# A hybrid decoder trunk: five value projections of the first layer moved behind the block inverse, the inverse traced in five parts

## The chip, the cores and the metric

The kernel runs on one core of a Trainium2 chip. The metric is the device time of one execution in microseconds. The engines are named as the profile names them: PE (TensorE; PEld is its weight load), DVE (VectorE), ACT (ScalarE), POOL (GpSimd) and SP (SyncE, whose queue issues the weight loads).

## What is computed

Two decoder layers over 512 positions of width 1024, each with a feed-forward block. The first layer's mixer is a gated DeltaNet with 8 heads, and the change lies in it:

```python
p = h @ w_in                                  # q, k, v, gate, and two rates per head
qkv = silu(causal_dwconv(qkv, conv_w))        # 4 taps
q, k = l2norm(q) * DK ** -0.5, l2norm(k)
Lmat = where(strict, einsum(kb, k) * decay, 0)            # kb = k * beta, per chunk
sol = triangular_solve(eye + Lmat, [v * beta, kb * exp(gc)])   # unit lower triangular
...                                           # state recurrence over the chunks
o = rmsnorm(o, onorm_g) * silu(gate)
return o @ w_out
```

The second layer is a sliding-window attention with sinks, and the work ends with an RMS norm. All of it is float32.

## The kernel before

Activations lie transposed, 128 channels on the partitions and 512 positions along the free axis. A weight matrix is cut into pieces of 128 output channels by 1024 inputs. For each piece, `weights` loads 512 KB into one of three `raw` buffers, ACT casts it to a rounded high part `whi`, and DVE subtracts to get the low part `wlo` (two buffers each). A projection of one piece is 24 products on PE: eight k-tiles of high weights with high and low activations, then eight of low weights with high activations. They accumulate in one of two PSUM tiles named `mm`; six more tiles, `sm`, serve all small products. `next_weights` keeps one further piece loaded and cast.

A piece's sums are evicted by `convolved`: DVE multiplies by R (`u`), ACT scales by the last tap, DVE adds three taps (line 234), ACT applies SiLU (line 634). A gate's piece needs only the eviction (line 650) and a SiLU. A key head (`k_head`) then has its own transposes and products, its decay and a copy of its diagonal blocks to `dg`. A value head (`v_head`) has four transposes on PE, with the value as their operand, and four scaled copies back on ACT, with the coefficients `c1`. The last key head calls `coefficients`, which makes `c1`, `c2n` and their kin on DVE.

`inverse` inverts all 32 by 32 diagonal blocks at once. DVE transposes `dg` into `lan`, POOL multiplies `lan` by the coefficients (line 605), and 31 rounds of one multiplication (line 613) and one addition (line 614) on DVE follow, each needing the one before. Then DVE transposes the result into `Tc` and `Uc` (lines 618 and 619). `place` copies `Uc` into the four diagonal strips of `U`, two on DVE and two on ACT (line 626). `level(h)` is a generator that builds the inverse of a 128 by 128 block of head h out of these, in five steps of small products; its first step copies a piece of `Tc` into `tm` on ACT (line 752), its second has the first matmuls (`tm` with `NT`), its third also needs `U`. Up to three heads are in flight.

The pieces are numbered in the text as `order` runs, from 0. Before, that is eight keys, then values 16, 17, gate 24, values 18, 19, gate 25, values 20, 21, gate 26, value 22, gate 27, value 23, gate 28: 21 pieces, so that piece 11 is value 18. In the middle of each piece from the seventh on, `follow(2)` runs up to two waiting heads, always leaving one. `inverse()` is traced whole after piece 13. Behind the pieces come `place()`, 12 products of the first query, 8 more, and the last value head. `queries` is a generator that yields after each product; it stops at a head's end until `level` has raised `solved` above that head. In the level loop `fill(early, 6)` draws six products after each step of a level.

What sets the order: a planner in the tile framework orders each engine's instructions by the priority of their tracing and by when it expects their inputs, and allocates buffers. `pin` keeps matmuls and transposes of this layer in the order in which they are traced. DVE, ACT and POOL are ordered by the planner. Engines wait for one another by semaphores. The level loop, which the diff does not print in full, is

```python
        while active or h < AH:
            if h < AH and len(active) < 3:
                active.append(level(h))
                h += 1
            for x in list(active):
                if next(x, 0) == 0:
                    active.remove(x)
                fill(early, 6)
```

Of the kernel before, what the change touches and what calls it, by code (L numbers as in the profile page):

```python
# [18 lines left out]
KT = D // P  # L19
NC = S // P  # L20
AH = 8
# [26 lines left out]
def tile_trunk(  # L48
# [48 lines left out]
    def mm(*args, **kw):  # L97
        pin(T.matmul(*args, **kw))  # L98
# [10 lines left out]
    def sm_tile():  # L109
        return psum[1].tile([P, S], F32, tag="sm", name="sm")  # L110
# [223 lines left out]
    with ExitStack() as phase:  # L334
# [3 lines left out]
        def row(tag, name):  # L338
            return dp.tile([P, S], F32, tag=tag, name=name, bufs=8)
# [24 lines left out]
        w_rates = w_rates[:, 0:KT * 48].rearrange("p (k n) -> p k n", n=48)  # L364
        nc.sync.dma_start(raw_ba[:, 0:P], w_ba)

        first_pieces = iter(range(8, 24)), iter(range(24, 29))
        order = [next(first_pieces[kind]) for kind in (0,) * 8 + (0, 0, 1, 0, 0, 1, 0, 0, 1, 0, 1, 0, 1)]
        sources = [w_in[n] for n in order + list(range(8)) + list(range(29, 32))] + [w_out[n] for n in range(KT)]
        ahead = []  # L370

        def next_weights():
# [147 lines left out]
        def squares(dst, h, src):  # L520
            junk = temp("junk")
            for c in range(NC):
                cs = slice(c * P, (c + 1) * P)
                A.activation(junk[:, cs], src[:, cs], AF.Square, accum_out=dst[:, h * NC + c:h * NC + c + 1])
# [11 lines left out]
        kT, kd, NT, vb, qT = [], [], [], [], []  # L536

        def transposed(x):
            pst = sm_tile()
            for c in range(NC):  # L540
                turn(pst[:, c * P:(c + 1) * P], x[:, c * P:(c + 1) * P], ident)
            return pst
# [27 lines left out]
        def q_head(h, q):  # L570

            squares(qss, h, transposed(q))
            pq = sm_tile()
            for c in range(NC):
                mm(pq[:, c * P:(c + 1) * P], kT[h][:, c * P:(c + 1) * P], q[:, c * P:(c + 1) * P], start=True, stop=True)
            V.tensor_tensor(DT[h], pq, DT[h], ALU.mult)
# [23 lines left out]
        def inverse():  # L600

            lan = big("lan", [P, 32, 32])
            V.transpose(lan, dg.rearrange("p hc i -> p i hc"))
            V.transpose(c2t, c2n)
            G.tensor_tensor(lan, lan, c2t.unsqueeze(2).to_broadcast([P, 32, 32]), ALU.mult)
            tmp = big("tmp", [P, 1024])
            tl = big("tl", [P, 32, 32])
            G.memset(tl, 0.0)
            V.memset(tl.rearrange("p a b -> p (a b)")[:, 0:1024:33], 1.0)
            for j in range(31):  # L610
                n = 31 - j
                tv = tmp[:, 0:n * (j + 1)].rearrange("p (i c) -> p i c", c=j + 1)
                V.tensor_tensor(tv, lan[:, j + 1:, j:j + 1].to_broadcast([P, n, j + 1]), tl[:, j:j + 1, 0:j + 1].to_broadcast([P, n, j + 1]), ALU.mult)  # L613
                V.tensor_tensor(tl[:, j + 1:, 0:j + 1], tl[:, j + 1:, 0:j + 1], tv, ALU.add)  # L614

            Tc = big("Tc", [P, HC, 32])
            Uc = big("Uc", [P, HC, 32])
            V.transpose(Tc, tl.rearrange("p i c -> p c i"))
            V.transpose(Uc.rearrange("p a b -> p (a b)"), tl.rearrange("p a b -> p (a b)"))
            G.memset(U, 0.0)  # L620
            Tinv.extend((Tc.rearrange("p c hc -> p hc c"), Uc.rearrange("p i hc -> p hc i")))

        def place():
            for q in range(4):
                qs = slice(32 * q, 32 * q + 32)
                (V.tensor_copy if q < 2 else A.copy)(U[qs, :, qs], Tinv[1][qs])

        unread, after, SG = [], [], []

        def convolved(ps, n, x):  # L630
            u = temp("u")
            V.tensor_tensor(u, ps, R, ALU.mult)
            conv(x, u, col("conv", 4 * n, 4), 4)
            A.activation(x, x, AF.Silu)
# [19 lines left out]
        def follow(n):  # L654
            for _ in range(min(n, len(after) - 1)):
                f, h, x = after.pop(0)
                f(h, x)
# [4 lines left out]
        solved = [0]  # L662

        def queries():
            waits = None
            for h in range(AH):
                w = next_weights()
                ps = mm_tile()
                for i in range(3 * KT):
                    if i == 18 and waits:  # L670
                        q_head(*waits)
                    products(ps, w, i, i + 1)
                    yield
                while solved[0] <= h:
                    yield
                qT.append(row("NT", "q"))
                convolved(ps, h, qT[-1])
                waits = (h, qT[-1])
            for _ in range(24):
                next(late, None)  # L680
                yield
            q_head(*waits)

        def gates():
            while len(SG) < AH:
# [8 lines left out]
        def fill(steps, n):  # L694
            for _ in range(n):
                next(steps, None)

        for i, n in enumerate(order):
            w = next_weights()
            if i == 0:  # L700
                products(ps_first, w, 2 * KT)
                unread.append((ps_first, n))
                continue
            ps = sm_tile() if i == 2 else mm_tile()
            products(ps, w, 0, 12)
            if i == 1:
                y = rms_mean(*parts)
            elif i == 2:
                rates()
            elif i == 6:  # L710
                gc_rows = sums()
            elif i > 6:
                if i == 6 + 1:
                    decays(range(4), gc_rows)
                follow(2)
            products(ps, w, 12)
            unread.append((ps, n))
            if i == 1:
                R = tpool.tile([P, S], F32, tag="R", name="R", bufs=1)
                A.copy(R, rms_bc(y))  # L720
                A.copy(ba, ps_ba[32:48, :])
                V.tensor_tensor(ba, ps_ba[:16, :], ba, ALU.add)
                V.tensor_tensor(ba, ba, R[:16, :], ALU.mult)
            elif i == 6 + 1:
                decays(range(4, 8), gc_rows)
            read()
            if i == 13:
                inverse()
        late = gates()
        early = queries()  # L730
        place()
        fill(early, 12)
        follow(1)
        fill(early, 8)
        after.append(None)
        follow(1)


        def pairs(x):
# [48 lines left out]
        active, h = [], 0  # L788
        while active or h < AH:
# [3 lines left out]
            for x in list(active):  # L793
                if next(x, 0) == 0:
                    active.remove(x)
                fill(early, 6)
        fill(early, 2 * AH * 3 * KT)


        St = None  # L800
# [116 lines left out]
        for m in range(KT):  # L917
            if m < 2:
                ps = two[m][0]
            else:  # L920
                w = next_weights()
                ps = mm_tile()
                for k in range(KT):
                    out_products(ps, w, k)
            h = hpool.tile([P, S], F32, tag="h", name="h")
# [13 lines left out]
    with ExitStack() as phase:  # L939
# [137 lines left out]
        ps, steps = q_steps(0)  # L1077
# [11 lines left out]
        for n in range(32 + 6):  # L1089
            if n < 32:  # L1090
                t, part = n // 4, n % 4
                if part == 0 and t < 7:
                    ps, steps = q_steps(t + 1)
# [11 lines left out]
        for m in range(KT):  # L1105
            hi, lo = weights(w_o[m], KT)
            ps = mm_tile()
# [76 lines left out]
```

## Time and profile before

| | us |
|---|---|
| three runs, median | 1239.77 |
| three runs, lowest and highest | 1237.69 and 1240.0 |
| the profiled execution | 1236.28 |
| its span, first to last instruction | 1234.6 |
| PE busy, of the span | 1215.3 |
| DVE busy, of the span | 822.3 |

All times in the rows are counted from the start of the span. A row of a timeline has the start, the duration, the engine, the line, the operation, what it writes and reads with the shape, and a count where equal instructions follow each other; what stands in square brackets is the engine's idle time before it and who ended it. Matmuls are pipelined: a row's duration is longer than the distance to the next matmul. The granted clock is a share of 2.4 GHz.

### The profile page before, as it was taken

To read this page: it belongs to the slowest core of one execution; us is meant where nothing else is said; L and a number is where in the kernel's file an instruction comes from. 1 tells how busy PE (TensorE), PEld (TensorE's weight loads), DVE (VectorE), ACT (ScalarE), POOL (GpSimd) and SP (SyncE) were. 2 spreads that over 40 slices of the span, in tenths; PEclk is the share of its full clock that TensorE was granted. 3 is DMA by queue.
4 is the path that set the end of the run, shared out by engine and by line. 5 is a ranking of instruction groups with operands and counts; after the bars stand their busy time and mean duration, and the time that the engine had idled before them with its cause. 6 is when DMAs were issued, how large, how long until landed. Compare 5 with 4: busy or idle time off the path is not lost.

```text
span 1234.6 us, 15981 instructions
## 1 busy us (share of the span) xinstructions
PE 1215.3 (98%) x6072; PEld 1008.5 (82%) x6072; DVE 822.3 (67%) x1430; ACT 585.6 (47%) x1146; POOL 50.5 (4%) x97
## 2 busy tenths in 40 slices
PE   9999989999999999999999999999999999999997
PEld 7887777897888888888888878888888888888887
DVE  6899955568586677675333689865876776762243
ACT  6664576465444444443222478754444444432231
POOL 1010000000000000000000003220000000000000
PEclk9999999999999999999999999999999999999999
DMA  5212211222333322332333321112333333333331
GB/s 204 86 51 81 90 52 52 69 70 69 103 92 96 102 90 99 103 96 83 97 99 102 104 74 42 45 49 89 99 89 102 103 87 102 102 89 100 94 94 69
DMA packets 33341, 108.69 MB, mean 88 GB/s; under 512 B 3824, under 2 KB 5360, under 8 KB 33264
## 3 DMA queue, kind: packets, MB, share of 16 engines
q1 hardware_dynamic: 32112, 106.66, 28.0%
q8 instruction: 48, 0.79, 0.3%
q10 hardware_dynamic: 1152, 1.01, 0.2%
q14 instruction: 29, 0.24, 0.1%
HBM read 105.56 MB, written 2.10 MB: 87 GB/s over the span
## 4 chain that ended last, share of the span: by engine, by line
PE 85%; DVE 10%; ACT 3%; issue 1%; DMA 0%; SPq 0%; DVEq 0%; ACTq 0%
PE mm L98 75%; PE sm L98 8%; DVE wlo L120 1%; PE sm L101 1%; DVE v L234 1%; DVE s L1032 1%; DVE tl L614 1%; DVE tmp L613 1%; ACT s L1040 1%; DVE q L1006 1%; DVE s L1043 1%; DVE s L1027 1%; DVE dg L561 0%; ACT whi L119 0%; DMA xk<-in_xT 0%
## 5 line engine op out<-in xcount | busy, mean ns | idle before, releaser
L98 PE MATMUL mm<-xh,whi 128*128 128x512 f32 x968 | 381.2, 394 | 0.0
L98 PE MATMUL mm<-xl,whi 128*128 128x512 f32 x968 | 377.8, 390 | 0.0
L119 ACT CAST whi<-raw 128x1024 fp32r<-128x1024 f32 (+1 forms) x192 | 198.4, 1034 | 357.8 <-PE mm L98 289.0
L120 DVE TENSOR_TENSOR wlo<-raw,whi 128x1024 fp32r<-128x1024 f32 (+1 forms) x192 | 230.0, 1198 | 107.7 <-PE mm L98 59.4
L98 PE MATMUL mm<-xh,wlo 128*128 128x512 f32 x968 | 242.0, 391 | 0.0
L98 PEld LDWEIGHTS mm<-xh,whi 128*128 128x128 f32 x968 | 182.0, 188 | 38.7 <-issue 0.6
L98 PEld LDWEIGHTS mm<-xl,whi 128*128 128x128 f32 x968 | 182.0, 188 | 36.7
L98 PEld LDWEIGHTS mm<-xh,wlo 128*128 128x128 f32 x968 | 181.2, 188 | 37.7
L234 DVE SCALAR_TENSOR_TENSOR y<-u,small,y 128x511 f32<-128x511 f32 (+1 forms) x176 | 131.3, 748 | 3.7 <-ACT y L231 0.7
L98 PE MATMUL mm<-gh,whi 128*128 128x512 f32 x330 | 129.3, 392 | 0.0
L98 PE MATMUL mm<-gl,whi 128*128 128x512 f32 x330 | 129.3, 392 | 0.0
L231 ACT ACTIVATE y<-u,small 128x512 f32<-128x512 f32 x88 | 71.7, 816 | 100.2 <-DVE u L269 100.2
L269 DVE TENSOR_TENSOR u<-mm,R 128x512 f32<-128x512 f32 x88 | 60.3, 687 | 71.1 <-PE mm L98 71.0
L98 PE MATMUL mm<-gh,wlo 128*128 128x512 f32 x330 | 82.8, 391 | 0.0
L98 PEld LDWEIGHTS mm<-gh,wlo 128*128 128x128 f32 x330 | 62.0, 188 | 13.6
L98 PEld LDWEIGHTS mm<-gl,whi 128*128 128x128 f32 x330 | 62.1, 188 | 13.4
L98 PEld LDWEIGHTS mm<-gh,whi 128*128 128x128 f32 x330 | 62.0, 188 | 13.5
L154 DVE TENSOR_TENSOR gl<-y,gh 128x512 fp32r<-128x512 f32 x44 | 30.5, 693 | 50.6 <-ACT gh L153 50.6
L285 DVE TENSOR_TENSOR h<-mm,h 128x512 f32<-128x512 f32 x15 | 10.4, 692 | 45.3 <-PE mm L98 45.3
L1056 POOL TENSOR_SCALAR_AFFINE_SELECT pT<-pT 128x256 f32<-128x256 f32 x64 | 29.8, 467 | 93.1 <-ACT pT L1054 90.8
L274 DVE TENSOR_TENSOR y<-y 128x512 f32<-128x512 f32 x44 | 30.5, 692 | 1.4
L273 ACT ACTIVATE y<-y 128x512 f32<-128x512 f32 x44 | 27.5, 625 | 2.1 <-DVE y L234 2.1
(298 smaller groups left out, 1519.1 us busy)
## 6 DMA issues: line engine op xcount, KB each, us to landing
raw<-in_w_up SPq DMA_DIRECT2D x88, 512.0 KB, 3.5
raw<-in_w_dn SPq DMA_DIRECT2D x32, 512.0 KB, 3.5
raw<-in_w_in SPq DMA_DIRECT2D x31, 512.0 KB, 3.5
raw<-in_w_dn SPq DMA_DIRECT2D x16, 384.0 KB, 3.1
raw<-in_w_out SPq DMA_DIRECT2D x8, 512.0 KB, 3.5
raw<-in_w_q SPq DMA_DIRECT2D x8, 512.0 KB, 3.5
raw<-in_w_o SPq DMA_DIRECT2D x8, 512.0 KB, 3.5
xk<-in_xT SPq DMA_DIRECT2D x8, 256.0 KB, 4.6
```

The costliest lines, as they stand in the source:

```text
L98: pin(T.matmul(*args, **kw))
L101: pin(T.transpose(out, x, eye))
L119: A.copy(hi[:, :w], raw[:, :w])
L120: V.tensor_tensor(lo[:, :w], raw[:, :w], hi[:, :w].bitcast(F32), ALU.subtract)
L154: V.tensor_tensor(lo, src, hi.bitcast(F32), ALU.subtract)
L231: A.activation(dst, u, AF.Identity, scale=last, bias=bias)
L234: V.scalar_tensor_tensor(dst[:, d:], u[:, :S - d], w[:, j:j + 1], dst[:, d:], ALU.mult, ALU.add)
L269: V.tensor_tensor(u, ps, R, ALU.mult)
L273: A.activation(cv[0], cv[0], AF.Silu)
L274: V.tensor_tensor(cv[0], cv[0], cv[1], ALU.mult)
L613: V.tensor_tensor(tv, lan[:, j + 1:, j:j + 1].to_broadcast([P, n, j + 1]), tl[:, j:j + 1, 0:j + 1].to_broadcast([P, n, j + 1]), ALU.mult)
L1056: G.affine_select(out=pT[:, x], in_=pT[:, 0], compare_op=ALU.is_ge, fill=0.0, base=x - 1, pattern=[[0, 2], [-sign, P]], channel_multiplier ...
```

## The change

The first layer's list of pieces ends after value 18 and five gates: keys 8 to 15, values 16 to 18, gates 24 to 28, 16 pieces. Values 19 to 23 become the first five pieces of the `queries` generator, with their heads (`v_head`) traced after the 18th product of the next piece, as the queries' own heads are. `inverse` becomes a generator with four stops, and its five parts are traced after the pieces 11 to 15, the five gates. The 12 and 8 products of the first query that stood between `place()` and the level loop are gone, and the one value head left is traced there. The number of products, and what each computes, stays the same.

```diff
-        first_pieces = iter(range(8, 24)), iter(range(24, 29))
-        order = [next(first_pieces[kind]) for kind in (0,) * 8 + (0, 0, 1, 0, 0, 1, 0, 0, 1, 0, 1, 0, 1)]
-        sources = [w_in[n] for n in order + list(range(8)) + list(range(29, 32))] + [w_out[n] for n in range(KT)]
+        order = list(range(8, 16)) + list(range(16, 19)) + list(range(24, 29))
+        sources = [w_in[n] for n in order + list(range(19, 24)) + list(range(8)) + list(range(29, 32))] + [w_out[n] for n in range(KT)]
...
                 V.tensor_tensor(tl[:, j + 1:, 0:j + 1], tl[:, j + 1:, 0:j + 1], tv, ALU.add)
+                if j % 7 == 6:
+                    yield
...
         def queries():
+
             waits = None
-            for h in range(AH):
+            for n in [*range(19, 24), *range(AH)]:
                 w = next_weights()
                 ps = mm_tile()
                 for i in range(3 * KT):
                     if i == 18 and waits:
-                        q_head(*waits)
+                        waits[0](*waits[1:])
                     products(ps, w, i, i + 1)
                     yield
-                while solved[0] <= h:
+                if n >= 16:
+                    v = row("vb", "v")
+                    convolved(ps, n, v)
+                    waits = (v_head, n - 16, v)
+                    continue
+                while solved[0] <= n:
                     yield
                 qT.append(row("NT", "q"))
-                convolved(ps, h, qT[-1])
-                waits = (h, qT[-1])
+                convolved(ps, n, qT[-1])
+                waits = (q_head, n, qT[-1])
             for _ in range(24):
                 next(late, None)
                 yield
-            q_head(*waits)
+            waits[0](*waits[1:])
...
-            if i == 13:
-                inverse()
+            if i >= 11:
+                if i == 11:
+                    inverting = inverse()
+                next(inverting, None)
         late = gates()
         early = queries()
+        for _ in inverting:
+            pass
         place()
-        fill(early, 12)
-        follow(1)
-        fill(early, 8)
         after.append(None)
-        follow(1)
+        follow(len(after))
...
-        fill(early, 2 * AH * 3 * KT)
+        fill(early, 3 * AH * 3 * KT)
```

## Rows read from the trace of the kernel before

**Rows 1.** The page: busy time of each engine, share, instructions.

```profile
PE 1215.3 (98%) x6072; PEld 1008.5 (82%) x6072; DVE 822.3 (67%) x1430; ACT 585.6 (47%) x1146; POOL 50.5 (4%) x97
```

**Rows 2.** Waits of PE, whole span: total us, times, longest.

```profile
PE sm L101 <- ACT v L634: 5.5, 3, 2.8
...
PE sm L98 <- DVE tm L761: 0.4, 1, 0.4
```

**Rows 3.** Windows: length, busy us and count by engine, granted clock, DMA.

```profile
core 0: us, PE busy (x) PEld busy (x) DVE busy (x) ACT busy (x) POOL busy (x), PEclk, DMA share, GB/s
...
110.00:145.00 35.00, 33.83 (x155) 27.73 (x154) 34.00 (x75) 15.89 (x29) 0.00 (x0) 1.00 0.30 90
...
160.00:242.00 82.00, 81.55 (x602) 65.18 (x601) 45.55 (x72) 46.33 (x139) 3.38 (x10) 1.00 0.18 58
```

**Rows 4.** Timeline of PE: starts of pieces, last value's transposes, first level.

```profile
89.75 0.39 PE L98 MATMUL mm<-xh,whi 128*128 128x512 f32 x1
...
109.28 0.39 PE L98 MATMUL mm<-xh,whi 128*128 128x512 f32 x1
...
114.72 0.39 PE L98 MATMUL mm<-xh,whi 128*128 128x512 f32 x1
...
120.66 0.39 PE L98 MATMUL mm<-xh,whi 128*128 128x512 f32 x1
...
158.22 0.66 PE L101 MATMUL sm<-const,v 128*128 128x128 f32 x4 [2.80 <-ACT v L634]
158.64 1.18 PE L98 MATMUL mm<-xh,wlo 128*128 128x512 f32 x4
159.65 0.81 PE L98 MATMUL sm<-tm,NT 128*96 128x64 f32 x8
```

**Rows 5.** DVE by line, 91.3 to 145.13: busy us, mean ns, idle before.

```profile
L234 DVE SCALAR_TENSOR_TENSOR v<-u,small,v 128x509 f32<-128x509 f32 (+2 forms) x15 | 11.2, 744 | 0.0
L120 DVE TENSOR_TENSOR wlo<-raw,whi 128x1024 fp32r<-128x1024 f32 x9 | 10.9, 1216 | 0.0
L614 DVE TENSOR_TENSOR tl<-tl,tmp 128x31 f32<-128x31 f32 (+15 forms) x31 | 10.6, 341 | 0.7
L613 DVE TENSOR_TENSOR tmp<-lan,tl 128x31 f32<-128x31 f32 (+15 forms) x31 | 10.5, 339 | 0.6
L632 DVE TENSOR_TENSOR u<-mm,R 128x512 f32<-128x512 f32 x5 | 3.4, 683 | 0.0
L650 DVE TENSOR_TENSOR u<-mm,R 128x512 f32<-128x512 f32 x4 | 2.7, 683 | 0.0
```

**Rows 6.** Timelines of POOL, DVE and ACT around the inverse.

```profile
99.71 1.92 POOL L605 TENSOR_TENSOR lan<-lan,c2t 128x1024 f32<-128x1024 f32 x1 [29.71 <-DVE t L164]
...
130.47 0.68 DVE L650 TENSOR_TENSOR u<-mm,R 128x512 f32<-128x512 f32 x1
131.07 0.40 DVE L613 TENSOR_TENSOR tmp<-lan,tl 128x240 f32<-128x240 f32 x1
...
145.13 2.09 DVE L618 STREAM_TRANSPOSE Tc<-tl 128x1024 f32<-128x1024 f32 x1
...
147.26 1.75 ACT L752 COPY tm<-Tc 32x128 f32<-32x128 f32 x4 [2.97 <-DVE Tc L618]
148.92 4.25 ACT L626 COPY U<-Uc 32x1024 f32<-32x1024 f32 x2
```

**Rows 7.** Windows at the end of the span, columns as in rows 3.

```profile
1227.00:1228.00 1.00, 0.84 (x8) 0.60 (x6) 0.80 (x5) 0.00 (x0) 0.00 (x0) 1.00 0.00 0
...
1233.00:1234.00 1.00, 0.00 (x0) 0.00 (x0) 0.00 (x0) 0.00 (x0) 0.00 (x0) 0.50 0.19 68
```

**Rows 8.** Timeline of PE, two of the kernel's first 512-column matmuls.

```profile
5.86 0.63 PE L98 MATMUL sm<-xh,w_rates 128*48 128x512 f32 x1 [0.59 <-DVE w_rates L386]
...
6.99 0.39 PE L98 MATMUL mm<-xl,whi 128*128 128x512 f32 x1
```

**Rows 9.** Timeline of PE in the level loop: a group of six products.

```profile
163.31 0.50 PE L98 MATMUL mm<-xh,whi 128*128 128x512 f32 x1
...
164.89 0.43 PE L98 MATMUL sm<-tm,U 32*32 32x32 f32 x8
```

## The prediction

> **What bounds the kernel now.** I read the page's engine shares first, then TensorE's own waits, then the stretch from 60 to 242 us by windows, and there the timelines of TensorE and VectorE. The shares say that TensorE (PE) is busy 98% of a span of 1234.6 us [rows 1], and the diff removes or adds no matmul. So time can only come from places where PE waits, or go to new ones. PE's list of waits names what this layer can give back: three waits of together 5.5 us on transposes of a value head, each time for the SiLU that ends that value's convolution, and one of 0.4 us in the first block of the inverse's levels [rows 2]. The longest, 2.80 us, is the last value's, at 158.22 [rows 4]. That is 5.9 us in all, and no more can be won here.
>
> The windows say what is behind those waits. From 110 to 145 us VectorE (DVE) is busy 34.0 of 35 us, PE 33.8; from 160 to 242 us DVE is busy only 45.6 of 82, ACT 46.3, and PE practically always [rows 3]. So DVE is the late engine until the inverse is done, and PE afterwards. DVE's work between 91.3 and 145.13 us, grouped by line, is 15 convolution steps, 9 subtractions for weight pieces, 62 steps of the inverse and 9 evictions [rows 5]. The inverse's steps stand there between the others, and none of those groups had more than 0.7 us of idle time ahead of it: DVE is a full queue, and the end of the inverse is the sum of what lies in front of it.
>
> **The change, part by part.** Pieces are numbered as `order` runs, from 0; pieces 0 to 9 and their companions do not change.
>
> *What PE does before the first level.* Before, PE starts piece 11 at 89.75 and the first matmul of a level (tm with NT) at 159.65: 69.90 us, of which 5.50 is waiting, so 64.4 us of work [rows 2, 4]. After, what stands in program order between the same two points is five gates, the transposes of three values and six products. One undisturbed piece of 24 products takes 114.72 - 109.28 = 5.44 us, a product 0.227; a piece with one value's transposes takes 120.66 - 114.72 = 5.94, so those cost 0.50, or about 0.35 where they follow other small matmuls [rows 4]. The sum is 5 x 5.44 + 0.50 + 0.35 + 0.40 + 6 x 0.227 + 0.1 for the switch = 29.9 us. PE stands in front of the first level at 89.75 + 29.9 = 119.7. The other 34.5 us of its work come behind.
>
> *When the first level can start.* It needs Tc, the transposed inverse, and four copies of it on ACT. Before, Tc starts at 145.13 (2.09 us) and the four copies at 147.26 take 1.75, so the operands are there at 149.0, 3.9 us after Tc's start [rows 6]. After, DVE has less in front of Tc. Four values (19 to 22) leave this stretch: 12 of the 15 convolution steps. Durations overlap by 0.08 us: the eviction at 130.47 lasts 0.68, and the next instruction starts after 0.60 [rows 6]. A convolution step of 0.744 us in the mean [rows 5] so counts 0.66, in all 7.9 us. Evictions go from 9 to 6 (one value, five gates): 3 x 0.60 = 1.8 us. Weight subtractions go from 9 to 6, since PE calls pieces 18 to 20 later: 3 x (1.216 - 0.08) = 3.4 us. That is 13.1 us, and Tc starts at 132.0; the first level at 135.9.
>
> *The new wait.* 135.9 - 119.7 = 16.2 us. Before, five value pieces more stood in this stretch, and 18 products more, those of the first query that the two removed `fill` lines put there. Since DVE is full, later or earlier evictions and casts shift nothing else in this sum. Its ends: if the planner runs the inverse ahead of everything that is not needed, it starts where POOL has finished lan, 99.71 + 1.92 = 101.6 [rows 6], takes 62 steps of 0.34 us and the gaps of 1.3 us, 22.4 us [rows 5], and must still let two subtractions and four evictions pass (4.7 us): Tc at 128.7, first level at 132.6, wait 12.9. If one more subtraction and two more evictions go first on DVE (2.3 us), it is 138.2 and 18.5.
>
> *Behind the wait.* Queued behind the blocked matmul on PE are the other levels and all products of the values and queries; nothing else on the chip can feed PE, so every microsecond goes into the total. POOL's clearing of the tm tiles waits for the inverse as before. SP's weight loads run three tiles ahead and then stand still until PE resumes. ACT copies two strips of U in 4.25 us [rows 6] directly behind the first level's operands; the third step of the level needs U, and PE reaches it after 0.6 + 2 x 1.5 us, so 0.6 us of waiting is in it.
>
> *The clock.* After PE's last matmul, at 1227 to 1228 us, the granted clock reads 1.00 (2.4 GHz), and by 1233 it reads 0.50 (1.2 GHz), with no matmul since 1227.8 [rows 7]. In the stretch with PE's longest waits, 2.8 us and less, it reads 1.00 throughout [rows 3]; a wait of 16 us is longer than PE's idleness before that low reading. Back at work the first 512-column matmuls would run at half speed: among the kernel's first matmuls one took 0.63 us at 5.86, and the same shape 0.39 at 6.99 [rows 8]. I estimate from these two rows up to 6 us at half speed, of which half is lost. With the 0.6 us for U, which a slow PE would not notice, I take 2.6 us; ends 0.6 and 2.9. The Trainium skill says the same in "TensorE: Matmul & The Clock Gate", Part 1: the clock starts low, sustained activity releases it, and an idle stretch puts it back; its section on oscillation warns of kernels that pay this at each gap. By that rule the 2.6 us are due; without it the sum would be 2.0 less. The end of this trace agrees with the fall.
>
> *Interleaving.* Six products between two small steps of a level take 164.89 - 163.31 = 1.58 us instead of 1.36 [rows 9]: 0.2 us for the switch. The level loop calls 40 groups of six. Before, 12 of them found the query generator waiting for `solved`, since 168 of the 240 calls became products; after, the values fill all 40. That is 12 x 0.2 = 2.4 us, less about 1.0 for value transposes that no longer split a piece: 1.4, ends 0 and 2.6.
>
> *What I cost at nothing.* The moved DVE and ACT work of five values (3 convolution steps, an eviction, a weight subtraction: about 4 us on DVE; scaling, SiLU, four scaled copies, a cast: 3.5 on ACT) goes to a stretch where both were busy a little over half [rows 3], and which grows by the same 34 us of PE work; at 20 us more each they stay below 66 of some 115. If that cover failed, a late SiLU would cost PE 1 to 3 us, as now [rows 2]. Tracing the inverse in five parts changes what a priority says, but its steps are interleaved already and DVE is full; it moves the time only inside the bounds above.
>
> **The sum.** -5.9 (old waits) + 16.2 (new wait) + 2.6 (clock, U) + 1.4 (switches) = +14.3 us. The profiled execution took 1236.28 us, 1.7 around its span; the three runs have a median of 1239.77, 0.28% more. By the profiled one the result is 1250.6, by the median 1254.1. I forecast 1254.
>
> **Rivals.**
> (a) The inverse runs ahead, or the clock stays up. With the early end of 12.9 us for the wait and the low ends of the clock, -5.9 + 12.9 + 0.6 + 1.4 gives +9.0, so 1249; with the profiled base and no switches, 1244. For it: the first parts of the inverse are traced earlier than any later gate. Against it: evictions and casts of the gates are traced earlier still. Chance 0.18.
> (b) More stands ahead of Tc, or value heads wait in the level loop as they do now: 18.5 instead of 16.2 and up to 2 us of SiLU waits: +18, 1258. Chance 0.10.
> (c) Not slower: products of the values overtake the blocked level on PE. Place: PE's queue behind the last gate. The two accumulators and two ready weight pieces would let 48 products go, and more as DVE evicts. It takes 16.2 + 1.4 - 5.9 = 11.7 us of cover, 52 products beyond the six, to reach the old time; if the whole 16.2 were covered, the result would be -4.5, 1235. Against it: `pin` keeps program order, and in the trace PE sat 2.80 us in front of the last transposes with four products of the same query ready right behind them [rows 4]. The Trainium skill, "TensorE: Matmul & The Clock Gate", Part 2, agrees: only weight loads are pulled ahead, matmuls stay in order. Chance 0.06.
> My own case has 0.66.
>
> **Range and chances.** Own case and (b) reach from 1249 to 1259, and (a) down to 1244; so 1244 to 1259. A measurement of this kernel can tell about 0.2% (2.5 us) from no change. Faster by more than that is two thirds of (c): 0.04; within it 0.02; slower 0.94.
>
> **What the new profile would show.** Right: one wait of PE of 13 to 18 us in front of the first tm matmul with NT, ended by ACT's copies of Tc, which end near 136; the three waits on value transposes gone; granted clock below 1.00 in the microseconds after it; the last 96 products in one run after the levels. Tc's start tells the DVE sum: 132 by mine, 129 if the inverse ran ahead. Wrong: if PE executes products between the last gate and the first level in numbers (case c), or if the stretch from the last gate to the levels is short because Tc starts before 120, which would mean that DVE's queue in front of the inverse was not what I counted.

## The result and the profile after

| | before | after |
|---|---|---|
| four runs of each, median, us | 1239.88 | 1256.91 |
| lowest and highest, us | 1237.69 to 1240.72 | 1256.59 to 1257.46 |
| the profiled execution, us | 1236.28 | 1257.46 |
| its span, us | 1234.6 | 1255.7 |

The changed kernel takes 1.0146 times as long, with a 95% interval of 1.0131 to 1.0161: 17.0 us more by the medians, 21.2 by the two profiled executions. The forecast was 1254, in a range of 1244 to 1259. One run of the kernel before, beside the last experiment, took 1302.98 us at a granted clock of 0.884 (a slow state), and no figure here uses it.

The page's engine shares after, for [rows 1]:

```profile
PE 1219.5 (97%) x6072; PEld 1009.3 (80%) x6072; DVE 823.6 (66%) x1430; ACT 586.2 (47%) x1146; POOL 52.4 (4%) x97
```

The counts are the same on every engine. PE is busy 4.2 us longer, and the span is 21.1 us longer: the change moved work, and PE now waits more. Where, its waits over the whole span say (total us, times, longest), for [rows 2]:

```profile
PE sm L98 <- issue: 17.0, 1, 17.0
PE sm L101 <- ACT q L635: 3.6, 3, 1.2
PE sm L98 <- DVE q L1014: 3.1, 4, 1.2
PE mm L98 <- DVE u L651: 1.3, 1, 1.3
...
PE sm L101 <- ACT v L635: 0.2, 1, 0.2
```

Of the 5.5 us on value transposes 0.2 are left. New are one wait of 17.0, one of 1.3 on a PSUM eviction, and three of 1.2 each on the SiLU of a query. (Line numbers shift with the edits: in the changed kernel the inverse's steps stand one line lower than before, Tc, U, evictions and SiLU one higher, the levels' copies of Tc eight higher.) PE's timeline after, the starts of pieces 11 and 14, the last of the six products in front of the first level, that level, products behind it, and one query's transposes, for [rows 4]:

```profile
91.10 0.39 PE L98 MATMUL mm<-xh,whi 128*128 128x512 f32 x1
...
109.78 0.47 PE L98 MATMUL mm<-xh,whi 128*128 128x512 f32 x1 [1.28 <-DVE u L651]
...
122.58 0.39 PE L98 MATMUL mm<-xl,whi 128*128 128x512 f32 x1
139.93 1.51 PE L98 MATMUL sm<-tm,NT 128*96 128x64 f32 x8 [16.96 <-issue]
...
142.19 0.63 PE L98 MATMUL mm<-xh,whi 128*128 128x512 f32 x1
...
144.75 0.43 PE L98 MATMUL mm<-xh,whi 128*128 128x512 f32 x1
...
237.02 0.66 PE L101 MATMUL sm<-const,q 128*128 128x128 f32 x4 [1.22 <-ACT q L635]
```

Nothing runs on PE between 122.97 and 139.93. The row of the wait names no releaser ("issue"); the copies of Tc that its matmul reads end at 138.16 + 1.67 = 139.83, in the timelines below. Behind the wait the 512-column products take 0.63 us, and 0.43 and less from 144.75. The windows show the clock (length, busy us and count by engine, granted clock, DMA), for [rows 3] and [rows 7]:

```profile
8.00:10.00 2.00, 1.64 (x5) 0.98 (x5) 1.62 (x3) 2.00 (x5) 0.00 (x0) 0.57 1.01 372
...
128.00:140.00 12.00, 0.07 (x1) 0.10 (x1) 11.18 (x27) 1.80 (x5) 1.29 (x3) 0.50 0.14 44
140.00:145.00 5.00, 5.00 (x17) 4.21 (x18) 2.00 (x4) 4.92 (x6) 2.38 (x4) 0.52 0.01 3
145.00:150.00 5.00, 5.00 (x39) 4.00 (x38) 1.44 (x4) 4.61 (x10) 0.00 (x0) 1.00 0.00 0
```

From 140 to 145 PE is busy without a gap at half its clock, and does 17 instructions; in the next five it does 39. The first of these rows is the kernel's start: this execution was at 0.57 there (before it was at 1.00), and reached piece 11 at 91.10 instead of 89.75. That is no work of the change; times of after below are also given less these 1.35 us.

What DVE does in front of Tc, grouped by line, from 92.66 to 136.2 (busy us, mean ns, idle before), for [rows 5]:

```profile
L613 DVE TENSOR_TENSOR tl<-tl,tmp 128x31 f32<-128x31 f32 (+15 forms) x31 | 10.6, 342 | 0.9
L612 DVE TENSOR_TENSOR tmp<-lan,tl 128x31 f32<-128x31 f32 (+15 forms) x31 | 10.6, 342 | 2.7 <-POOL lan L604 1.8
L120 DVE TENSOR_TENSOR wlo<-raw,whi 128x1024 fp32r<-128x1024 f32 x6 | 7.3, 1220 | 0.0
L651 DVE TENSOR_TENSOR u<-mm,R 128x512 f32<-128x512 f32 x5 | 3.4, 684 | 0.0
L234 DVE SCALAR_TENSOR_TENSOR v<-u,small,v 128x509 f32<-128x509 f32 (+2 forms) x3 | 2.2, 742 | 0.0
...
L633 DVE TENSOR_TENSOR u<-mm,R 128x512 f32<-128x512 f32 x1 | 0.7, 684 | 0.0
```

Three convolution steps, six subtractions, six evictions: the counts of the prediction. What was not in it is the idle time in front of the inverse's steps, 3.6 us where it was 1.3 [rows 5]. Its main piece, and the end of the chain, stand in the timelines of POOL, DVE and ACT, for [rows 6]:

```profile
103.88 2.95 POOL L604 TENSOR_TENSOR lan<-lan,c2t 128x1024 f32<-128x1024 f32 x1 [32.53 <-DVE c L586]
...
103.82 1.23 DVE L120 TENSOR_TENSOR wlo<-raw,whi 128x1024 fp32r<-128x1024 f32 x1
106.86 0.21 DVE L612 TENSOR_TENSOR tmp<-lan,tl 128x31 f32<-128x31 f32 x1 [1.82 <-POOL lan L604]
...
136.21 1.92 DVE L619 STREAM_TRANSPOSE Tc<-tl 128x1024 f32<-128x1024 f32 x1
...
138.16 1.67 ACT L760 COPY tm<-Tc 32x128 f32<-32x128 f32 x4 [10.44 <-DVE Tc L619]
```

POOL's product begins 2.8 us later than before (like for like), takes 2.95 us instead of 1.92, and DVE stands idle for it. The eviction that PE waited 1.28 us for stood behind this wait and eight steps of the inverse in DVE's order: it ran at 108.95, though the products that it reads had ended at 103.1. The first matmul of a level follows Tc's start by 3.7 us; its operands took 3.9 before.

**The account of the spans.** 1.35 us are the start. Waits: 16.96 + 1.28 + 0.2 + 3.6 less the old 5.9 are +16.1. Half clock over some 4.8 us of work is +2.4. About 0.8 to 1.1 are left for the switches, and 0.5 elsewhere (the later wait at L1014 is 3.1 us and was 2.6). Together 21.1.

### The profile page after: what moved, and what is told of

Its sections match the earlier page's. It is cut to its first block, busy times and chain, and to the rows that moved or that the text cites. A ratio compares the mean times of both kernels' runs of the same rounds, so it can differ in the third digit from the quotient of the medians.

```text
span 1255.7 us, 15969 instructions
## 1 busy us (share of the span) xinstructions
PE 1219.5 (97%) x6072; PEld 1009.3 (80%) x6072; DVE 823.6 (66%) x1430; ACT 586.2 (47%) x1146; POOL 52.4 (4%) x97
## 3 DMA queue, kind: packets, MB, share of 16 engines
q10 hardware_dynamic: 1152, 1.01, 0.2%
## 4 chain that ended last, share of the span: by engine, by line
PE 86%; DVE 9%; ACT 2%; issue 1%; DMA 0%; POOL 0%; SPq 0%; DVEq 0%; ACTq 0%
PE mm L98 77%; PE sm L98 8%; PE sm L101 1%; DVE wlo L120 1%; DVE s L1040 1%; DVE tl L613 1%; DVE tmp L612 1%; ACT s L1048 1%; DVE s L1051 1%; DVE q L1014 1%; DVE s L1035 1%; DVE v L234 0%; DVE dg L560 0%; ACT whi L119 0%; DMA xk<-in_xT 0%
## 5 line engine op out<-in xcount | busy, mean ns | idle before, releaser
L269 DVE TENSOR_TENSOR u<-mm,R 128x512 f32<-128x512 f32 x88 | 60.3, 687 | 71.1 <-PE mm L98 71.1
L98 PEld LDWEIGHTS mm<-gh,whi 128*128 128x128 f32 x330 | 62.0, 188 | 13.5
L98 PEld LDWEIGHTS mm<-gl,whi 128*128 128x128 f32 x330 | 62.0, 188 | 13.5
L633 DVE TENSOR_TENSOR u<-mm,R 128x512 f32<-128x512 f32 x23 | 15.8, 688 | 25.8 <-PE mm L98 25.7
```

## The experiments

My theory after this: the five values were cover. In program order they stood in front of the first level, and PE worked on them while DVE finished the inverse; without them PE waits, one microsecond for each lost, and a low clock behind that. Each ratio below is to runs of the kernel before on the same chip, whose medians were 1238.0 to 1238.3. The four runs of the changed kernel were made apart from these, so what a variant of it gained is read from its ratio too: only the one with half the inverse stands clear of the changed kernel's 1.0146 [1.0131, 1.0161], and for the others the waits in the traces carry the reading. The rivals: that the clock is the larger part; that the inverse in five parts, or the query waits behind the loop, cost it; that the loss is in the amount of work left in the loop.

**Half of the inverse left out.** The last 15 of the 31 rounds are gone, so the blocks are not fully inverted; all else is the changed kernel.

```diff
-            for j in range(31):
+            for j in range(16):
```

> The changed kernel with 16 of the 31 rounds of the inverse: the last 15 rounds are left out, so the blocks are not fully inverted. The 30 steps left out take 122.6 to 136.2 us less two evictions and two subtractions, 10 us of DVE. Theory (wait ended by DVE's sum): the first level starts 10 us earlier, wait 7 us, 1246.9, and 1244.5 if the clock stays up. Rival (the wait is ended by something else, POOL, ACT or a buffer): 1255 or more.

Measured: 1243.41 us, 1.0042 times before [1.0027, 1.0057], 13.5 less than the changed kernel. PE's timeline of it, the last product and the first level:

```profile
121.52 0.39 PE L98 MATMUL mm<-xl,whi 128*128 128x512 f32 x1
126.14 0.86 PE L98 MATMUL sm<-tm,NT 128*96 128x64 f32 x8 [4.23 <-POOL tm L756]
```

The wait fell from 16.96 to 4.23 us, by 12.7, and the time by 13.5: what DVE saves ahead of Tc, the kernel saves whole. (The row names POOL's clearing of tm, which had ended by 123.2; ACT's copies of Tc ended at 126.04, 0.1 us before the matmul.) It is more than the 10 us expected, since the last gate's eviction (125.38) and one subtraction (128.16) came behind Tc (122.43) here. The clock still fell, a little later: the windows read 1.00 from 122 to 127 and 0.66 from 127 to 132, so some 1.7 us were lost to it instead of 2.4, the other 0.7. The path is inverse, then first level, then everything.

**The removed products alone, taken from the kernel before.** 

```diff
-        fill(early, 12)
-        follow(1)
-        fill(early, 8)
         after.append(None)
```

> The kernel before with the other small part alone: the 20 products between place() and the level loop are gone, pieces and inverse stay. Theory (PE's order is fixed, what stood in front of a blocked instruction was its cover): the last value's transposes still wait for the SiLU that DVE's queue ends at the same time, so that wait grows from 2.8 to about 7.3 us; the 20 products come later at full price: 1239 + 4.5 = 1243.5. Rival (the level loop finds those products a place where PE waited anyway): 1239.

Measured: 1243.64 us, 1.0034 times before [1.0021, 1.0048], 5.4 us more. PE in front of the last value's transposes, for the 2.80 of [rows 4]:

```profile
157.69 1.11 PE L101 MATMUL sm<-const,v 128*128 128x128 f32 x4 [7.05 <-ACT v L634]
```

20 products, 4.5 us of work, fewer in front of it; 4.25 us more of waiting. So products in front of a waiting instruction are worth about their own length, by a second experiment. The 5.4 us of time are not that alone: in this trace the clock also fell, to 0.50 from 155 to 160 us and 0.63 from 160 to 165, where the kernel before read 1.00.

**20 products put back in the changed kernel,** between the last gate and the levels.

```diff
         place()
+        fill(early, 20)
         after.append(None)
```

> The changed kernel (1256.9 us) with 20 products of the first value put back between place() and the level loop. Theory (the loss is PE's wait for the inverse, which is the start of the first level less PE's arrival): 20 x 0.227 = 4.5 us more cover, none of it brings work to DVE, the wait falls from 17.0 to 12.5 us, the clock still falls in it: 1252.4. Rival (the loss is the value work in the level loop, the wait would have come anyway): 1257.

Measured: 1254.28, 1.0127 times before [1.0112, 1.0142], 2.6 us less than the changed kernel. PE's timeline, and DVE by line up to Tc (92 to 138.1 us):

```profile
141.85 1.51 PE L98 MATMUL sm<-tm,NT 128*96 128x64 f32 x8 [15.01 <-issue]
```

```profile
L120 DVE TENSOR_TENSOR wlo<-raw,whi 128x1024 fp32r<-128x1024 f32 x7 | 8.5, 1218 | 0.0
L234 DVE SCALAR_TENSOR_TENSOR v<-u,small,v 128x509 f32<-128x509 f32 (+2 forms) x6 | 4.5, 743 | 0.0
```

My expectation held that none of the 20 brings work to DVE. It was wrong: with the six that the loop draws they are 26, two more than complete value 19. So its eviction, its three convolution steps (six now, not three) and one more subtraction (seven, not six) came in front of Tc, 3.7 us of DVE work, and 4.5 us of cover bought only 1.95 of the wait. The rest of the gain is one query wait less (2.4 us in two, not 3.6 in three).

**72 products put back.** The same line with 72; the value heads then stand in another order in the list of heads, so that heads get each other's values and the output is another; the operations are the same.

```diff
         place()
+        fill(early, 72)
         after.append(None)
```

> The changed kernel with 72 products, three value pieces, before the level loop. They are 16.3 us of PE work. Theory: DVE is full, and the pieces bring 2 evictions, 6 convolution steps and 2 weight subtractions in front of Tc, 7.5 us; so the wait is 17.0 - 16.3 + 7.5 = 8.2 us, the time 1256.9 - 8.8 = 1248, or 1246 if the clock stays up in 8 us. Rival (DVE puts the inverse first, the values' work behind): wait about 1 us, clock up, 1238.

Measured: 1252.69, 1.0118 times before [1.01, 1.0135], 4.2 us less. PE's waits and timeline:

```profile
PE sm L101 <- ACT v L635: 14.8, 4, 8.6
```

```profile
135.62 1.11 PE L101 MATMUL sm<-const,v 128*128 128x128 f32 x4 [5.68 <-ACT v L635]
...
152.59 1.11 PE L101 MATMUL sm<-const,v 128*128 128x128 f32 x4 [8.65 <-ACT v L635]
```

16.3 us of products were back, but the wait did not go: it moved to the transposes of the values, whose convolutions share DVE with the inverse. Both experiments say the same: a value's piece is 5.4 us of cover on PE and some 4 us of work on DVE, the late engine. A gate's piece brings only an eviction and a subtraction there, 1.7 us by the same count, so gates should be the better cover; both kernels place five of the eight in front of the levels, and no run tried more.

**Is it the clock?** Two kernels put products into a PSUM tile that nobody reads, between the last gate and the levels: 60, then 74. They are added to the work, take the place of waiting and keep PE busy.

```diff
+        idle = sm_tile()
+        for i in range(60):
+            mm(idle, xg[0][:, 0, 0:P], xg[0][:, 0, :], start=(i == 0), stop=(i == 59))
```

> The changed kernel with 60 matmuls of 512 columns into an unused PSUM tile just before the level loop, which only keep PE busy (13.6 us) in the wait; no result depends on them. Theory: the first level starts when it did, the granted clock stays at 1.00, and the 2.4 us that the low clock cost come back: 1254.5. Rival (the low clock fell on stretches that wait anyway): 1256.9.

```diff
+        idle = sm_tile()
+        for i in range(74):
+            mm(idle, xg[0][:, 0, 0:P], xg[0][:, 0, :], start=(i == 0), stop=(i == 73))
```

> The changed kernel with 74 matmuls into an unused PSUM tile in the wait (16.8 us), where 60 left a gap of 3.4 us and the clock fell once more behind it. Theory (the low clock behind the wait costs 2.4 us): the granted clock stays at 1.00, the level's first small matmul starts at the same distance from Tc, and the time is 1254.5. Rival (the low clock falls on a stretch that ACT and DVE bound): 1257, PE waiting in front of the second head's first matmul instead.

Measured: 1257.44 (1.0151 [1.0134, 1.0167]) and 1256.27 (1.0136 [1.0113, 1.0158]), against 1256.91 without. Windows of the one with 60, then of the one with 74, and the latter's third level step:

```profile
142.00:144.00 2.00, 2.00 (x7) 1.52 (x6) 0.22 (x1) 1.98 (x2) 0.04 (x1) 0.50 0.00 0
```

```profile
142.00:144.00 2.00, 2.00 (x10) 1.35 (x8) 0.53 (x2) 1.99 (x2) 0.18 (x1) 1.00 0.00 0
```

```profile
144.00 0.43 PE L98 MATMUL sm<-tm,U 32*32 32x32 f32 x8
```

With 60 a wait of 3.4 us was left, and the clock fell behind it all the same; nothing was gained. With 74 (0.4 us left) it stayed at 1.00. That third step then started 7.55 us after Tc (which started at 136.45), where in the changed kernel it was 9.60 (145.81 after 136.21). So the low clock costs 2.05 us in that place, near the 2.4 of the account; 0.5 came back as a longer SiLU wait. The whole kernel gained only 0.6 by the medians, which its runs do not separate from nothing; from the start of piece 11 to the end of the span the trace is 1.6 us shorter (1163.0 for 1164.6), as 2.05 less 0.5 would have it. Here the clock is the small part.

**The heads five products later,** for the query waits behind the loop.

```diff
-                    if i == 18 and waits:
+                    if i == 23 and waits:
```

> The changed kernel with each value's and query's head traced after 23 products of the next piece instead of 18. Behind the level loop it waits three times 1.2 us for the SiLU of a query, because 18 products in one run (4.1 us) are shorter than that query's chain through DVE and ACT. Theory: 5 x 0.227 = 1.1 us more cover each, the three waits shrink from 3.6 to about 0.3 us, 1253.6. Rival (the waits move to the next product that needs them): 1256.9.

Measured: 1255.58, ratio to before 1.0135 [1.0111, 1.016]. The three waits of 1.2 us are gone from its trace. From the first level to the last matmul it takes 1105.49 us (141.65 to 1247.14), the changed kernel 1108.12 (139.93 to 1248.05): 2.6 less. Of the medians 1.3 is to be seen, less than the intervals can hold apart. That these waits are on the path is shown in the trace, and their price end to end stays between 1 and 3 us.

**The inverse in five parts, alone,** in the kernel before.

```diff
                 V.tensor_tensor(tl[:, j + 1:, 0:j + 1], tl[:, j + 1:, 0:j + 1], tv, ALU.add)
+                if j % 7 == 6:
+                    yield
...
-            if i == 13:
-                inverse()
+            if i >= 11:
+                if i == 11:
+                    inverting = inverse()
+                next(inverting, None)
```

> The kernel before with one part of the change alone: the inverse traced in five parts after the pieces 11 to 15; the order of the pieces and the fills stay. Theory (DVE is full there, its sum in front of Tc sets the end, and the parts change only who passes whom): within 2 us of 1239. Rival (the earlier trace lets the inverse run ahead and is what the change lives from): 1234 or less, with Tc's start before 141.

Measured: 1239.36, 1.0011 [0.9993, 1.0028], the same three value waits, 5.4 us. In the kernel before it does nothing that the runs can tell: DVE is full there, as the prediction said. In the changed kernel, as built, the planner gives every engine the same order of instructions whether the inverse is traced in five parts or whole behind piece 11; whole behind piece 13, as before, DVE's order differs, and no run has that.

**Fewer values moved.** One value, and two, behind the inverse instead of five, with that value's products in front of the levels (`fill`), and heads later in their pieces. The list of pieces and the fill of each, in the kernel before (cut; the generator of values and queries is as in the change):

```diff
+        order = list(range(8, 16)) + [16, 17, 24, 18, 19, 25, 20, 21, 26, 22, 27, 28]
...
+            cut = 12 if i < 11 else 22
...
+        fill(early, 24)
```

> The kernel before with one value, the last, moved in front of the queries as the change does with five, a fill of 24 products between place() and the levels, value heads after 22 products from piece 11 on and heads of values and queries after 23 products in the generator. Theory (cover must fit the DVE sum: PE comes to the first level at about 149, when Tc's copies end, and no SiLU is waited for): of before's 5.9 us of waits 1.5 stay, 1238.5 - 4.4 = 1234. Rival (each cover moves the wait to the next instruction that DVE or ACT ends, as in the run with late heads): 1238 to 1241.

```diff
+        order = list(range(8, 16)) + [16, 17, 24, 18, 19, 25, 20, 26, 21, 27, 28]
...
+            cut = 12 if i < 11 else 22
...
+        fill(early, 48)
```

> The same with two values, 22 and 23, in front of the queries and a fill of 48. Theory: DVE has one value less in front of Tc, 2.6 us, so Tc comes earlier by up to that, PE comes to the first level at 149 as well; 1234, and 1232 if no wait is left. Rival: 1238 to 1241.

Measured: 1243.74 (1.0035 [1.0022, 1.0047]) and 1244.67 (1.0047 [1.0034, 1.0059]). The waits of the first and PE's timeline of the second:

```profile
PE sm L98 <- DVE tm L765: 6.0, 2, 5.5
```

```profile
158.24 1.11 PE L101 MATMUL sm<-const,v 128*128 128x128 f32 x4 [9.76 <-ACT v L633]
```

With one value moved, DVE's copy into tm stands behind a weight subtraction that waits 4.29 us for ACT's cast; ACT, late by the copies of U (150.75 to 154.81), has a SiLU, four scaled copies and four copies of Tc to do before it. With two, Tc starts earlier (143.74), but the moved value's own convolution then comes behind the inverse and PE waits for its SiLU. Neither was faster than before: of the orders tried, the old one had the smaller waits.

**Only the last value's head moved,** into the level loop, to save the 2.80 us of [rows 4] with all products kept; and the same with the four strips of U copied by DVE.

```diff
-            products(ps, w, 0, 12)
+            cut = 12 if i < 11 else 22
+            products(ps, w, 0, cut)
...
-        after.append(None)
-        follow(1)
...
+            if h == 3 and len(after) == 1 and after[0]:
+                after.append(None)
+                follow(1)
```

> The kernel before with its value heads later: from piece 11 on a value's transposes follow 22 products of the next piece instead of 12, and the last value's head stands in the level loop, after the second head has begun. Pieces, fills and inverse stay. Theory (the 5.5 us of waits before are all that there is to win, and they end with the SiLU of a value whose convolution DVE makes late): these waits vanish, PE comes to the first level at 154, after Tc's copies at 149: 1239 - 5 = 1234. Rival (DVE's queue is what ends, and the wait moves to the first level or to U): 1238 to 1240.

```diff
-                (V.tensor_copy if q < 2 else A.copy)(U[qs, :, qs], Tinv[1][qs])
+                V.tensor_copy(U[qs, :, qs], Tinv[1][qs])
```

> The kernel before with its value heads later (as in the run with late heads) and all four strips of U copied by DVE (1.1 us each) instead of two by ACT (2.1 us each). In the run with late heads ACT was busy with these copies from 150.9 to 155.0, and behind them stood the last value's scaling and a cast, for which DVE waited 3.5 us, and behind DVE the first level's tm, for which PE waited 2.8 us. Theory (ACT's queue behind Tc is the bound there): ACT is free 4.2 us earlier, DVE has 2.2 us more, PE's waits behind 150 fall from 4.0 to about 2 us: 1240.5 - 2 to 3 = 1238, no slower than the kernel before, at best 1236. Rival (any reordering there moves the wait): 1240 to 1242.

Measured: 1240.5 (1.0012 [0.9999, 1.0025]) and 1241.47 (1.0018 [1.0002, 1.0033]). The two largest new waits of PE in the first, then in the second:

```profile
PE sm L98 <- DVE tm L760: 2.8, 1, 2.8
...
PE mm L98 <- DVE u L632: 1.2, 1, 1.2
```

```profile
PE sm L98 <- DVE tm L760: 3.8, 1, 3.8
...
PE mm L98 <- DVE u L632: 1.2, 1, 1.2
```

The three value waits are gone in both, and PE waits for a level's copy into tm and for an eviction instead. In the first the last value's scaling stands on ACT behind the copies of U, by ACT's timeline:

```profile
150.87 4.13 ACT L626 COPY U<-Uc 32x1024 f32<-32x1024 f32 x2
155.03 0.73 ACT L229 ACTIVATE v<-u,small 128x512 f32<-128x512 f32 x1
```

In the second DVE, busy for 9.1 of the 10 us from 150 on, has these copies too and is later still. The 5.5 us of value waits are the face of DVE and ACT being late; moving the head changes which operation shows it.

The waits alone do not give the loss of these two. Over the whole list PE waits 1.2 us less in the first than in the kernel before and 0.9 less in the second, yet from the start of piece 11 to the end of the span their traces take 1146.8 and 1150.8 us, against 1144.9. In both the granted clock fell behind the moved wait: 0.77 and 0.55 in the two stretches of 5 us from 160 on in the first, 0.57, 0.50 and 0.56 in the three of the second, with PE mostly at work. It fell at the same place in the traces with one and two values moved, and not in the trace of the kernel before [rows 3]. So a good part of what these orders lose is the clock, and no run takes that apart from the order.

## Why the prediction was right

The sign and the mechanism came out, and the time: +17.0 us by the medians for +14.3 said, 1256.9 for 1254. Between the two traces the change costs 19.8 us (21.1 less the 1.35 of the start), so the sum is 5.5 short; that the time lies closer is luck in part, as the point on the base says.

- **Old waits, −5.9.** 5.3 of the 5.5 on values went, and the 0.4 too. Right.
- **The new wait, 16.2.** It is 16.96, one wait, at the place named, 0.1 us behind the end of ACT's copies of Tc; half of the inverse less took 12.7 of it and 13.5 off the time. Both of its ends were later than said. PE arrived at 121.6 (122.97 less 1.35), not 119.7: 1.28 of that is the wait for the eviction of a gate, which stood behind steps of the inverse. Tc started at 134.9, not 132.0, though the counts of DVE's work were exact. DVE waited 1.82 us for POOL's product. And the 18 instructions that left had stood between steps of the inverse, each of which needs the one before, and cost less there than the sum said. DVE's timeline of the kernel before, then of the changed one:

```profile
127.71 0.41 DVE L613 TENSOR_TENSOR tmp<-lan,tl 128x252 f32<-128x252 f32 x1
128.04 0.74 DVE L234 SCALAR_TENSOR_TENSOR v<-u,small,v 128x510 f32<-128x510 f32 x1
128.70 0.42 DVE L614 TENSOR_TENSOR tl<-tl,tmp 128x252 f32<-128x252 f32 x1
```

```profile
123.05 0.42 DVE L613 TENSOR_TENSOR tl<-tl,tmp 128x256 f32<-128x256 f32 x1
123.50 0.42 DVE L612 TENSOR_TENSOR tmp<-lan,tl 128x255 f32<-128x255 f32 x1
```

A step with a convolution step behind it takes 0.99 us, alone 0.45: the convolution step costs 0.54, not the 0.66 of the sum. Read the same way, an eviction and a subtraction come out about 0.13 lower too, so for 18 instructions 2.3 us, an estimate from these rows, were not saved. Against these 4.1 us stands 1.3 saved where POOL no longer held up a small step (last section); the rest, 2.8, is the miss. So the overlap in the price of a DVE instruction was mis-sized, and the step "Since DVE is full, later or earlier evictions and casts shift nothing else in this sum" failed twice. In this one wait the two misses nearly cancelled, which is luck: with the 1.28 PE waits 18.2 us there, 2.0 more than said.

- **The clock and U, 2.6.** The clock fell, PE worked 4.8 us at half of it, 2.4 lost by the account, 2.05 by the run that kept it up; and U cost no wait, since the slow PE came later. Right.
- **Switches, 1.4.** 0.8 to 1.1 by what the account leaves; no run took them alone, so this is argued, not shown.
- **Costed at nothing.** This term was mis-sized. The prediction itself priced it at 1 to 3 us if a SiLU came late; it was 3.6, three times 1.2. The values now fill the loop, so the last 96 products, 72 of three queries and 24 of a gate, stand behind it in one run; 18 products there take 4.1 us, and a query's eviction, scaling, three convolution steps and SiLU take longer. With the heads five products later these waits were gone.
- **The parts of the inverse, nothing.** Right in the kernel before, by a run of their own; not run apart in the changed kernel.
- **The base.** To the profiled execution the forecast was 1250.6 and the profiled result 1257.46, so the trace is 6.9 us above the sum: 3.6 for the queries, 1.28 for the eviction, 0.76 for the longer first wait, 1.35 for the start, the rest small terms of both signs. To the medians only 2.8 are missing, since the four runs of before lie 1.4 to 4.4 us above its profiled execution. The sum was worked from that execution, one of the fastest, and then added to a median 3.5 us higher; the higher base covered for half of what the sum lacked. That is luck.

Rival (b), more ahead of Tc and late value heads, named a time of 1258, and a wait of 18.5, that lie closer, but neither of its causes is in the trace: DVE's counts were those of my own case, and the value heads in the loop wait 0.2 us. Rival (c), products passing the blocked level, is excluded: PE did nothing for 17 us in front of that level.

## What to carry to other kernels

Work in front of an instruction that waits is cover, and taking it away costs its length: before moving it, find which engine ends the wait and whether the moved work lies on that engine. Count for each covering product what it completes, since finishing a piece gives work to the late engine and lengthens the very wait that it covers. And when a loop's filler changes, look at what is left in one run behind the loop: there the latency of one element's chain, hidden until then, has only the next piece to hide in. Where two orders of one kernel are compared, read the granted clock behind every moved wait as well: fewer waits with a fall behind one of them can take longer.

## What was not expected of the hardware

**The clock falls after short waits, in some executions.** In the run with the inverse in five parts, a wait of 2.95 us was followed by half clock from 159 us on, with PE at work: its timeline and windows are

```profile
159.50 1.11 PE L101 MATMUL sm<-const,v 128*128 128x128 f32 x4 [2.95 <-ACT v L636]
```

```profile
161.00:163.00 2.00, 2.00 (x10) 1.66 (x9) 0.64 (x1) 1.98 (x5) 0.00 (x0) 0.50 0.68 244
...
167.00:169.00 2.00, 2.00 (x11) 1.72 (x11) 1.01 (x4) 0.72 (x1) 0.00 (x0) 0.50 0.62 231
```

It read 0.66 from 171 to 173. In the profiled execution of the kernel before, the same wait, of 2.80 there, was followed by a clock of 1.00 from 160 on [rows 3, 4]. Runs of the kernel before went from 1235.9 to 1243.9 us, those of the changed kernel within 0.9 us; that the one falls now and then and the other each time fits both. The mean granted clock of each run goes with it: in the experiments the 12 runs of the kernel before at 0.999 took 1235.9 to 1237.1 us, the 11 at 0.992 or 0.993 took 1241.8 to 1243.9, and the changed kernel's four read 0.990 each. In the trace with the five parts the waits are those of the kernel before, and from the start of piece 11 to the end it takes 1150.0 us for 1144.9: about 5 us for a low clock behind one short wait. The Trainium skill, "TensorE: Matmul & The Clock Gate", Part 1, says that the moment at which the clock is released differs from run to run of the same kernel; here it is the fall that comes in one execution and not in another.

**POOL and DVE hold each other up.** POOL's product of lan began at 103.88 after, while DVE's subtraction was running (103.82 to 105.05), and took 2.95 us. Before, it began at 99.71, took 1.92 [rows 6], and a small step of DVE that began inside it took 1.46 us, where the same kind of step takes 0.18 (and this one 0.18 after, with no product of POOL beside it); DVE's timeline of the kernel before:

```profile
100.21 1.46 DVE L165 SCALAR_TENSOR_TENSOR t<-t 128x32 f32<-128x32 f32 x1
...
102.73 0.18 DVE L166 SCALAR_TENSOR_TENSOR c<-t,c 128x32 f32<-128x32 f32 x1
```

Whoever began first ran at its own pace and the other ended after it. The Trainium skill, "SBUF — State Buffer", section "SBUF: two separate sides", says that the two engines share one pair of ports as an exclusive lock, which a DVE operation with two SBUF inputs takes against a GpSimd operation that reads SBUF; both traces agree. In the changed kernel this 1.0 us stands in front of the inverse, on the path.
